# Three-operation rotary embeddings, and small tables moved from VectorE to GpSimd

## The chip, the cores and the metric

The kernel runs on one core of one Trainium2 chip. The metric is the device time of one execution in microseconds (us). Before the change it is 2278.96 us, the median of three runs (2276.32 to 2279.6).

The engines are named as in the profile: PE is TensorE's matmul, PEld its weight load, DVE is VectorE, ACT is ScalarE, POOL is GpSimd, SP is SyncE, which here issues the loads of weights. Each engine works through its own instructions in a fixed order.

## The reference

A decoder trunk of two layers over 256 rows of 2048 columns, in float32. One layer computes

```
h = RMSNorm(x)
[u | ret q,k,v,g | nsa q, 3 x (k,v), gates | diff q,k,v] = h @ W_in
x = x + concat[S5(u), Retention(q,k,v,g), NSA(q,...), DiffAttn(q,k,v)] @ W_out
x = x + relu(RMSNorm(x) @ W1)^2 @ W2
```

S5 is a state-space scan, the other three mixers are causal attentions with four heads of 128. The queries and keys get rotary embeddings:

```
ang = pos * theta ** (-arange(0, d, 2) / d)
rope(x) = [x1 * cos(ang) - x2 * sin(ang), x2 * cos(ang) + x1 * sin(ang)]
```

with x1 and x2 the two halves of a head. The retention's q and k and NSA's q have four heads of 128, the differential attention's q and k have eight heads of 64, and NSA's three keys (compressed, selected, window) have a single head of 128. The differential attention also needs one constant a layer, lambda = exp(sum(lq1 * lk1)) - exp(sum(lq2 * lk2)) + lam_init.

## The kernel before

The 256 rows are two row tiles (`NT` = 2) of 128 rows. Every large product goes through `product` (L157): for a block of 512 output columns it loads the weights in chunks of 128 x 1024 (`raw`, by SP's queue), ACT rounds a chunk to its high part (`wh`, L153), DVE subtracts to get the low part (`wl`, L154), and PE does twelve matmuls for it: eight with `wh` (L172, L173) and four with `wl` (L177). There are three buffers for `wh` and two for `wl`. So all through the kernel both ACT and DVE have one full chunk of work for each twelve matmuls.

A layer begins with `mixers` (L839): eleven products with W_in (u, then q, k, v of the differential attention, NSA's q and its key/value blocks with the gates, the retention's q, k, v, g), and between them the attentions and the S5 states (`s5_pair`, eight calls a layer, shared out over the steps by `PACE`). Everything that the mixers need of elementwise work lies on DVE and ACT, between the chunks. Then W_out and the two products of the MLP follow, with little elementwise work beside them.

The order of the instructions of each engine is laid by the framework's scheduler: it simulates the program, and takes what is ready by its place in the program, with blocks under `hp()` moved up by 350 places. That order is fixed when the program is built.

What the change touches:

- `rope` (L377 to L392): the rotary embedding of one row tile. It does five DVE operations: source times cos over the full width (L388), each half of the heads times sin into a scratch tile `rtmp` (L389, L390), and the subtraction and the addition into the two halves of the destination (L391, L392). It is called for both row tiles by `diff_tr`, `nsa_qt` and `ret_tr` (512 columns, five times a layer), and by `rope1_tr` for each single-head key (128 columns, three times a layer).
- `rope1_tr` (L658): ropes a single-head key of both row tiles, transposes them on PE and copies them out.
- `nsa_kv` (L635) and the `kcv` tiles (L883 on): copies of the key and value columns out of PSUM, one tile for each row tile.
- `rope_tables` (L280): cos and sin of all angles, 128 x 128 elements, once at the start: the angles, their turns (`turns`, L97) on DVE, then Sin on ACT (L295, L297).
- `diff_lambda` (L343): the constant `nlam` of each layer with `exp_small` (L118) on 4 columns.

POOL has little to do before: the causal masks and `rsqrt` (L81), a chain of fourteen small operations that gives each norm. Between the evacuation of u's product and the first head norm it has none.

Of the kernel before, what the change touches and what calls it, by code (L numbers as in the profile page):

```python
# [54 lines left out]
class Trunk:  # L55
# [18 lines left out]
    # ---------------------------------------------------------------- helpers  # L74
# [6 lines left out]
    def rsqrt(self, dst, v, n, tag):  # L81
        """dst = 1/sqrt(v + eps) on [rows, n] float32 columns, by Newton steps on GpSimd"""
# [11 lines left out]
    def rnd(self, dst, src):  # L94
        self.nc.vector.tensor_scalar(dst, src, MAGIC, -MAGIC, ALU.add, ALU.add)

    def turns(self, th, n):  # L97
        """th radians -> f1, f2 with f1 + f2 = th/(2 pi) less a whole number, |f1 + f2| <= 1/2."""
        V = self.nc.vector
# [6 lines left out]
        self.rnd(b, a)  # L106
# [4 lines left out]
        V.scalar_tensor_tensor(a, h, I2P[2], a, ALU.mult, ALU.add)  # L111
        V.tensor_tensor(f2, f2, a, ALU.add)
        V.tensor_tensor(a, f1, f2, ALU.add)
        self.rnd(b, a)
# [3 lines left out]
    def exp_small(self, dst, x, n):  # L118
        """dst = exp(x) to float32 rounding on few columns."""
        V = self.nc.vector  # L120
# [4 lines left out]
        V.scalar_tensor_tensor(r, k, -LN2_HI, r, ALU.mult, ALU.add)  # L125
        V.scalar_tensor_tensor(r, k, -LN2_LO, r, ALU.mult, ALU.add)
# [8 lines left out]
        V.scalar_tensor_tensor(dst, p, 1.0, e, ALU.add, ALU.mult)  # L135

    # ------------------------------------------------------- weights and products
# [19 lines left out]
    def product(self, chunks, lhs, n=512, before=None):  # L157
        """sum over k of lhs[k]^T @ w[k]; chunks hold two k each. Returns the PSUM tiles of both row tiles."""
# [36 lines left out]
    def to_slots(self, src, cols, slots, j0, gain=None):  # L195
        """src(t): token-major [128, >=cols] tiles; transposes cols into slot pairs from j0 on."""
# [83 lines left out]
    def rope_tables(self, posi, invf):  # L280
        nc = self.nc
        V = nc.vector
        posf = self.T(NT)
        V.tensor_copy(posf, posi)
        ang = self.T(NT * 64)
        for t in range(NT):
            V.tensor_scalar(ang[:, t * 64:(t + 1) * 64], invf, posf[:, t:t + 1], None, ALU.mult)
        f1, f2 = self.turns(ang, NT * 64)
        V.tensor_tensor(f1, f1, f2, ALU.add)
        self.rnd(f2, f1)  # L290
        V.tensor_tensor(f1, f1, f2, ALU.subtract)
# [69 lines left out]
    # ---------------------------------------------------------------- norm of the residual  # L361
# [14 lines left out]
    # ---------------------------------------------------------------- rotary and head norms  # L376
    def rope(self, dst, src, t, heads, d):  # L377
        """dst, src: [128, heads * d] token-major; dst must not be src."""
# [5 lines left out]
        tb = lambda tab: tab[:, t, ::step][:, None, :]  # L384
# [36 lines left out]
    def head_tr(self, src, dst, engine):  # L421
        """src(t): token-major [128, 4 * 128]; dst [128, 2, 4, 128] (row tile, head, row)"""
# [29 lines left out]
    def s5_table(self, i):  # L452
        """[128, 2, 256]: cos and sin of t * theta for the state column i."""
# [36 lines left out]
    def s5_pair(self, i):  # L490
        """pairs i and i + 1: the inputs go to the frame that rotates with theta, are summed there with
# [600 lines left out]
```

## Time and profile before

| | |
|---|---|
| median of three runs | 2278.96 us |
| profiled execution, first to last instruction (span) | 2274.8 us |
| PE busy | 2249.3 us (99%) |
| DVE busy | 1411.6 us (62%) |
| ACT busy | 1083.1 us (48%) |
| POOL busy | 144.7 us (6%) |

For the profiled execution the profile gives the span alone; the median of the timed runs is 4.2 us above it.

How to read it: the shares are means over stages with different limits. Each matmul's record lasts from its issue to the end of its result, so that the records of neighbours overlap and PE's share is high by nature. In the mixers (0 to 365 us and 1168 to 1505 us) DVE is much busier than in the rest. The same holds for DVE's records: an operation's record is longer than the distance to the next one's start in a full queue, and that distance is what the operation costs the queue.

### The profile page before, as it was taken

The numbers are of one execution on the slowest core, as the hardware profiler recorded it, in microseconds if no ns is written. First come the engines' busy times: TensorE is split into PE (matmuls) and PEld (weight loads), VectorE is DVE, ScalarE is ACT, GpSimd is POOL, SyncE is SP. The second block draws the span as 40 slices with busy tenths as digits, with TensorE's granted clock in tenths as the row PEclk, the third lists the DMA queues.
The fourth block names the chain that finished last, engine by engine and source line by source line (L and its number), as shares of the span: only waits on it lengthen the run. The fifth ranks groups of instructions, "written<-read, shape, count | busy, mean of one in ns | idle before, by whom it ended". The sixth has DMA issues, their size and how long they took to land.

```text
span 2274.8 us, 29209 instructions
## 1 busy us (share of the span) xinstructions
PE 2249.3 (99%) x10732; PEld 1831.1 (80%) x10732; DVE 1411.6 (62%) x2105; ACT 1083.1 (48%) x1410; POOL 144.7 (6%) x396
## 2 busy tenths in 40 slices
PE   8999999999999999999999999999999999999999
PEld 7777778888888888888877777888888888888887
DVE  8988975555555555455569997566554554555554
ACT  6456554544344344344545664445444443443443
POOL 0213111000000000000002212010000000000000
PEclk9999999999999999999999999999999999999999
DMA  7544735555655555555554456355555556556554
GB/s 252 165 133 130 241 113 167 183 182 191 194 185 192 190 192 185 195 186 185 186 175 155 131 152 206 120 178 183 186 192 189 190 181 201 187 190 191 191 194 167
DMA packets 115919, 409.62 MB, mean 180 GB/s; under 512 B 14016, under 2 KB 14272, under 8 KB 115776
## 3 DMA queue, kind: packets, MB, share of 16 engines
q1 hardware_dynamic: 113184, 405.06, 53.8%
q10 hardware_dynamic: 2592, 2.70, 0.3%
q8 instruction: 84, 1.38, 0.2%
q14 instruction: 59, 0.48, 0.1%
HBM read 405.61 MB, written 2.10 MB: 179 GB/s over the span
## 4 chain that ended last, share of the span: by engine, by line
PE 86%; DVE 7%; POOL 3%; issue 2%; ACT 2%; DMA 1%; DVEq 0%; ACTq 0%; SPq 0%
PE mm L177 27%; PE mm L172 27%; PE mm L173 27%; DVE wl L154 2%; PE tp L203 2%; DVE w L515 1%; PE glu L551 1%; POOL rst L89 1%; PE bu L502 1%; PE nsc L759 0%; PE yp L530 0%; PE npv L769 0%; POOL rst L91 0%; POOL rst L90 0%; PE cmp L693 0%
## 5 line engine op out<-in xcount | busy, mean ns | idle before, releaser
L153 ACT ACTIVATE wh<-raw 128x1024 fp32r<-128x1024 f32 (+1 forms) x752 | 790.5, 1052 | 1055.0 <-PE mm L173 944.7
L154 DVE TENSOR_TENSOR wl<-raw,wh 128x1024 fp32r<-128x1024 f32 (+1 forms) x752 | 908.0, 1213 | 594.5 <-PE mm L177 557.6
L172 PE MATMUL mm<-wh,Al 128*128 128x512 f32 (+1 forms) x1728 | 670.1, 389 | 1.9 <-ACT wh L153 1.5
L173 PE MATMUL mm<-wh,Ah 128*128 128x512 f32 (+1 forms) x1728 | 669.1, 388 | 0.0
L172 PE MATMUL mm<-wh,Bl 128*128 128x512 f32 x1280 | 498.4, 389 | 0.9 <-DVE Bl L213 0.9
L173 PE MATMUL mm<-wh,Bh 128*128 128x512 f32 x1280 | 498.4, 389 | 0.0
L177 PE MATMUL mm<-wl,Ah 128*128 128x512 f32 (+1 forms) x1728 | 466.9, 391 | 10.9 <-DVE wl L154 10.5
L177 PEld LDWEIGHTS mm<-wl,Ah 128*128 128x128 f32 x1728 | 316.0, 188 | 88.4 <-DVE wl L154 18.4
L172 PEld LDWEIGHTS mm<-wh,Al 128*128 128x128 f32 x1728 | 325.1, 188 | 73.2 <-issue 4.6
L173 PEld LDWEIGHTS mm<-wh,Ah 128*128 128x128 f32 x1728 | 325.2, 188 | 69.7 <-issue 5.6
L177 PE MATMUL mm<-wl,Bh 128*128 128x512 f32 x1280 | 344.2, 391 | 0.2 <-DVE wl L154 0.2
L172 PEld LDWEIGHTS mm<-wh,Bl 128*128 128x128 f32 x1280 | 240.3, 188 | 51.1 <-DVE Bl L213 1.1
L173 PEld LDWEIGHTS mm<-wh,Bh 128*128 128x128 f32 x1280 | 240.3, 188 | 49.7
L177 PEld LDWEIGHTS mm<-wl,Bh 128*128 128x128 f32 x1280 | 238.6, 188 | 49.0 <-DVE wl L154 0.6
L934 DVE TENSOR_TENSOR x<-mm,x 128x512 f32<-128x512 f32 x96 | 61.8, 686 | 105.5 <-PE mm L177 105.5
L213 DVE TENSOR_TENSOR Bl<-tp,Bh 128x512 fp32r<-128x512 f32 x76 | 52.1, 687 | 70.9 <-ACT Bh L212 70.9
L86 POOL TENSOR_SCALAR rv<-rv 128x2 f32<-128x2 f32 x4 | 1.0, 244 | 879.8 <-DVE rv L372 879.8
L987 ACT ACTIVATE hid<-mm,rb 128x512 f32<-128x512 f32 x64 | 40.6, 685 | 24.2 <-PE mm L177 24.2
L212 ACT ACTIVATE Bh<-tp 128x512 fp32r<-128x512 f32 x76 | 40.8, 584 | 5.7 <-PE tp L203 5.7
L988 DVE TENSOR_TENSOR hid<-hid 128x512 f32<-128x512 f32 x64 | 41.2, 684 | 0.0
L515 DVE TENSOR_TENSOR_SCAN w<-mag,z 128x256 f32<-128x256 f32 x64 | 40.7, 678 | 0.0
L218 DVE SCALAR_TENSOR_TENSOR Al<-tp,gains,Ah 128x256 fp32r<-128x256 f32 x64 | 29.3, 478 | 16.9 <-ACT Ah L217 16.9
(300 smaller groups left out, 1187.4 us busy)
## 6 DMA issues: line engine op xcount, KB each, us to landing
raw<-in_w_dram SPq DMA_DIRECT2D x512, 512.0 KB, 3.4
raw<-in_w_main_dram SPq DMA_DIRECT2D x160, 512.0 KB, 4.0
raw<-in_w_out_dram SPq DMA_DIRECT2D x64, 512.0 KB, 3.6
aux<-in_wcmp_dram SPq DMA_DIRECT2D x16, 512.0 KB, 5.2
raw<-in_w_gate_dram SPq DMA_DIRECT2D x16, 268.0 KB, 2.6
x<-in_x_dram SPq DMA_DIRECT2D x8, 256.0 KB, 5.1
aux<-in_s5g_dram SPq DMA_DIRECT2D x4, 512.0 KB, 4.8
out_dram<-x ACTq DMA_DIRECT2D x8, 256.0 KB, 2.1
```

The costliest lines, as they stand in the source:

```text
L153: self.nc.scalar.activation(h[:, :cols], r[:, :cols], AF.Copy)
L154: self.nc.vector.tensor_tensor(l[:, :cols], r[:, :cols], h[:, :cols].bitcast(F32), ALU.subtract)
L172: nc.tensor.matmul(acc[t], rows(xl, t), mov(wh, j), start=k == 0, stop=False)
L173: nc.tensor.matmul(acc[t], rows(xh, t), mov(wh, j), start=False, stop=False)
L177: nc.tensor.matmul(acc[t], rows(lhs[k][0], t), mov(wl, j), start=False, stop=k == nk - 1)
L203: nc.tensor.transpose(pt[:, kk, t * P:(t + 1) * P], src(t)[:, c:c + P], self.ident)
L212: nc.scalar.activation(h, pt, AF.Copy)
L213: nc.vector.tensor_tensor(l, pt, h.bitcast(F32), ALU.subtract)
L515: V.tensor_tensor_scan(w[:, c, :], mg, z[:, c, :], 0.0, ALU.mult, ALU.add)
L934: self.nc.vector.tensor_tensor(x, acc[t], x, ALU.add)
L987: nc.scalar.activation(h, acc[t], AF.Relu, scale=r[:, t:t + 1])
L988: V.tensor_tensor(h, h, h, ALU.mult)
```

## The change

The sine table gets twice the width, with the sign of each half in it: -sin for the first, +sin for the second. `rope` then does three operations over the full width: source times cos, the source with its halves swapped (a reversed step in the access pattern) times the signed sine, and their sum. `rope1` does the same three operations for the two row tiles of a single-head key at once; for that the key tiles of both row tiles become one tile (`ko`, `kcv`, `k1r`). In `rope_tables` and `diff_lambda` the elementwise work goes from DVE to POOL, the two row sums of `diff_lambda` excepted. [...] Docstrings and comments are dropped; that part is left out here.

```diff
-    def rnd(self, dst, src):
-        self.nc.vector.tensor_scalar(dst, src, MAGIC, -MAGIC, ALU.add, ALU.add)
+    def rnd(self, dst, src, V=None):
+        (V or self.nc.vector).tensor_scalar(dst, src, MAGIC, -MAGIC, ALU.add, ALU.add)
+
+    def mul_add(self, V, dst, a, k, b, t):
+        if V is self.nc.vector:
+            V.scalar_tensor_tensor(dst, a, k, b, ALU.mult, ALU.add)
+        else:
+            V.tensor_scalar(t, a, k, None, ALU.mult)
+            V.tensor_tensor(dst, t, b, ALU.add)
...
     def turns(self, th, n, V=None):
+        V = V or self.nc.vector
...
-        V.scalar_tensor_tensor(f2, h, I2P[1], f2, ALU.mult, ALU.add)
+        self.mul_add(V, f2, h, I2P[1], f2, c)
...
     def rope_tables(self, posi, invf):
-        V = nc.vector
+        G = nc.gpsimd
...
-        f1, f2 = self.turns(ang, NT * 64)
+        f1, f2 = self.turns(ang, NT * 64, G)
...
-        self.rs = self.cst.tile([P, NT, 64], F32, name="rs")
-        nc.scalar.activation(fl(self.rs), f1, AF.Sin, scale=TWO_PI)
+        self.rs = self.cst.tile([P, NT, 2, 64], F32, name="rs")
+        nc.scalar.activation(self.rs[:, :, 0, :], t3(f1), AF.Sin, scale=-TWO_PI)
+        nc.scalar.activation(self.rs[:, :, 1, :], t3(f1), AF.Sin, scale=TWO_PI)
...
     def diff_lambda(self, dl):
-        V = nc.vector
+        V = nc.gpsimd
...
-            V.tensor_reduce(sm[:, 2 * l:2 * l + 2], dl[:, l, 0::2, :], AX, ALU.add)
-        self.exp_small(ex, sm, n * 2)
+            nc.vector.tensor_reduce(sm[:, 2 * l:2 * l + 2], dl[:, l, 0::2, :], AX, ALU.add)
+        self.exp_small(ex, sm, n * 2, V)
...
     def rope(self, dst, src, t, heads, d):
-        cosb = tb(self.rc)[:, :, None, :].to_broadcast([P, heads, 2, h])
-        sinb = tb(self.rs).to_broadcast([P, heads, h])
+        cosb = self.rc[:, t, ::step][:, None, None, :].to_broadcast([P, heads, 2, h])
+        sinb = self.rs[:, t, :, ::step][:, None, :, :].to_broadcast([P, heads, 2, h])
         V.tensor_tensor(o, s, cosb, ALU.mult)
-        V.tensor_tensor(m[:, :, 0, :], s[:, :, 1, :], sinb, ALU.mult)
-        V.tensor_tensor(m[:, :, 1, :], s[:, :, 0, :], sinb, ALU.mult)
-        V.tensor_tensor(o[:, :, 0, :], o[:, :, 0, :], m[:, :, 0, :], ALU.subtract)
-        V.tensor_tensor(o[:, :, 1, :], o[:, :, 1, :], m[:, :, 1, :], ALU.add)
+        V.tensor_tensor(m, s[:, :, ::-1, :], sinb, ALU.mult)
+        V.tensor_tensor(dst, dst, tmp, ALU.add)
+
+    def rope1(self, dst, src):
+        V = self.nc.vector
+        tmp = self.wk.tile([P, 512], F32, name="rtmp", bufs=1)[:, :SEQ]
+        v4 = lambda x: x.rearrange("p t (b c) -> p t b c", b=2)
+        s, o, m = v4(src), v4(dst), tmp.rearrange("p (t b c) -> p t b c", t=NT, b=2)
+        V.tensor_tensor(o, s, self.rc[:, :, None, :].to_broadcast([P, NT, 2, 64]), ALU.mult)
+        V.tensor_tensor(m, s[:, :, ::-1, :], self.rs, ALU.mult)
+        V.tensor_tensor(o, o, m, ALU.add)
...
     def nsa_kv(self, acc, kcol, r, tag):
+        k = self.wk.tile([P, NT, P], F32, name="ko", tag="ko" + tag, bufs=1)
...
-                ko = self.wk.tile([P, P], F32, name="ko", tag="ko" + tag, bufs=2)
-                nc.scalar.activation(ko, acc[t][:, kcol * P:(kcol + 1) * P], AF.Copy, scale=r[:, t:t + 1])
+                nc.scalar.activation(k[:, t, :], acc[t][:, kcol * P:(kcol + 1) * P], AF.Copy, scale=r[:, t:t + 1])
...
     def rope1_tr(self, k, tag):
-        for t in range(NT):
-            o = self.wk.tile([P, P], F32, name="k1r", bufs=2)
-            self.rope(o, k[t], t, 1, P)
-            nc.tensor.transpose(pt[:, t * P:(t + 1) * P], o, self.ident)
+        o = self.wk.tile([P, NT, P], F32, name="k1r", bufs=1)
+        self.rope1(o, k)
+        for t in range(NT):
+            nc.tensor.transpose(pt[:, t * P:(t + 1) * P], o[:, t, :], self.ident)
...
-            kv = [self.wk.tile([P, 2 * P], F32, name="kcv", tag="ev", bufs=4) for _ in range(NT)]
+            kv = self.wk.tile([P, NT, 2 * P], F32, name="kcv", tag="ev", bufs=4)
```

`exp_small` takes the engine as `turns` does; on POOL its three multiply-and-add steps become two operations each.

## Rows read from the trace of the kernel before

**Rows 1.** The page: busy us, share, instructions; then a group: count, busy, mean ns, idle.

```profile
PE 2249.3 (99%) x10732; PEld 1831.1 (80%) x10732; DVE 1411.6 (62%) x2105; ACT 1083.1 (48%) x1410; POOL 144.7 (6%) x396
...
L154 DVE TENSOR_TENSOR wl<-raw,wh 128x1024 fp32r<-128x1024 f32 (+1 forms) x752 | 908.0, 1213 | 594.5 <-PE mm L177 557.6
```

**Rows 2.** Busy us of each engine (instructions) by stage, granted clock, DMA share, GB/s.

```profile
0.00:365.00 365.00, 351.44 (x1851) 271.65 (x1852) 306.13 (x733) 206.03 (x342) 67.64 (x192) 1.00 0.52 168
365.00:1168.00 803.00, 803.00 (x3645) 667.05 (x3644) 432.86 (x442) 361.80 (x417) 8.34 (x28) 1.00 0.57 189
1168.00:1505.00 337.00, 329.45 (x1782) 257.14 (x1781) 269.28 (x535) 181.15 (x284) 64.00 (x162) 1.00 0.47 152
```

**Rows 3.** The same view in windows of 20 us, some of both mixers.

```profile
40.00:60.00 20.00, 20.00 (x98) 15.50 (x98) 20.00 (x56) 8.84 (x14) 0.00 (x0) 1.00 0.56 178
80.00:100.00 20.00, 17.88 (x75) 13.52 (x73) 18.92 (x35) 10.42 (x15) 3.32 (x9) 0.91 0.46 138
...
1180.00:1200.00 20.00, 18.55 (x78) 13.61 (x79) 19.93 (x35) 10.25 (x14) 0.00 (x0) 1.00 0.40 127
...
1420.00:1440.00 20.00, 20.00 (x96) 15.42 (x96) 10.42 (x29) 9.15 (x12) 2.92 (x3) 1.00 0.34 110
```

**Rows 4.** Who waited for whom, whole span: us in total, times, longest.

```profile
PEld mm L177 <- DVE wl L154: 18.9, 22, 2.3
PE mm L177 <- DVE wl L154: 10.7, 14, 1.8
```

**Rows 5.** DVE in order of time, single stretches: start us, us, what.

```profile
84.19 0.69 DVE L388 TENSOR_TENSOR drp<-evr,rc 128x512 f32<-128x512 f32 x1
84.79 0.69 DVE L517 TENSOR_TENSOR sc<-w,cs 128x512 f32<-128x512 f32 x1
...
1358.66 0.22 DVE L392 TENSOR_TENSOR k1r<-k1r,rtmp 128x64 f32<-128x64 f32 x1
1358.79 0.28 DVE L388 TENSOR_TENSOR k1r<-ko,rc 128x128 f32<-128x128 f32 x1
1358.99 0.42 DVE L681 TENSOR_TENSOR xp<-vcT,pe 128x256 f32<-128x256 f32 x1
1359.33 0.22 DVE L389 TENSOR_TENSOR rtmp<-ko,rs 128x64 f32<-128x64 f32 x1
```

**Rows 6.** DVE at the start: the tables' first operation, a later one, one of lambda.

```profile
8.88 0.16 DVE L284 CAST scr<-posi 128x2 f32<-128x2 int32 x1
...
23.03 0.21 DVE L95 TENSOR_SCALAR scr<-scr 128x128 f32<-128x128 f32 x1
23.16 0.17 DVE L122 TENSOR_SCALAR scr<-scr 128x32 f32<-128x32 f32 x1
...
34.51 0.15 DVE L125 SCALAR_TENSOR_TENSOR scr<-scr 128x4 f32<-128x4 f32 x1
34.58 0.17 DVE L130 TENSOR_SCALAR scr<-scr 128x32 f32<-128x32 f32 x1
```

**Rows 7.** ACT in order of time, where it takes the tables over.

```profile
25.79 0.32 ACT L295 ACTIVATE rs<-scr 128x128 f32<-128x128 f32 x1 [0.54 <-DVE scr L291]
...
26.64 1.05 ACT L153 ACTIVATE wh<-raw 128x1024 fp32r<-128x1024 f32 x1
```

**Rows 8.** POOL in order of time, the first head norm: first and last operations.

```profile
70.74 1.17 POOL L86 TENSOR_SCALAR hv<-hv 128x16 f32<-128x16 f32 x1 [46.53 <-DVE hv L406]
...
78.53 0.20 POOL L91 TENSOR_SCALAR rst<-rst 128x16 f32<-128x16 f32 x1
78.81 0.22 POOL L92 TENSOR_TENSOR hc<-hc,rst 128x16 f32<-128x16 f32 x1
```

**Rows 9.** POOL and DVE in order of time, a mask beside a chunk's low part.

```profile
301.49 0.64 POOL L563 TENSOR_SCALAR_AFFINE_SELECT np<-np 128x512 f32<-128x512 f32 x1 [1.76 <-ACT np L761]
301.64 1.56 DVE L154 TENSOR_TENSOR wl<-raw,wh 128x1024 fp32r<-128x1024 f32 x1 [0.28 <-ACT np L761]
```

**Rows 10.** DVE in order of time, the first differential query's norm.

```profile
79.07 1.29 DVE L410 TENSOR_TENSOR evr<-evr,hc 128x512 f32<-128x512 f32 x2 [2.49 <-POOL hc L92]
```

More of the change, by code (lines that the diff above doesn't have):

```diff
@@ L92, in rsqrt, with turns @@
             G.tensor_tensor(dst, dst, t, ALU.mult)
-    def rnd(self, dst, src):
-        self.nc.vector.tensor_scalar(dst, src, MAGIC, -MAGIC, ALU.add, ALU.add)
-    def turns(self, th, n):
-        V = self.nc.vector
+    def rnd(self, dst, src, V=None):
[6 more added lines that the diff above has]
+            V.tensor_tensor(dst, t, b, ALU.add)
+    def turns(self, th, n, V=None):
+        V = V or self.nc.vector
         c, h, l, a, b, f1, f2 = (self.T(n) for _ in range(7))
@@ L105, in turns, with exp_small @@
         V.tensor_scalar(a, h, I2P[0], None, ALU.mult)
-        self.rnd(b, a)
+        self.rnd(b, a, V)
         V.tensor_tensor(f1, a, b, ALU.subtract)
         V.tensor_scalar(f2, l, I2P[0], None, ALU.mult)
-        V.scalar_tensor_tensor(f2, h, I2P[1], f2, ALU.mult, ALU.add)
+        self.mul_add(V, f2, h, I2P[1], f2, c)
         V.tensor_scalar(a, l, I2P[1], None, ALU.mult)
-        V.scalar_tensor_tensor(a, h, I2P[2], a, ALU.mult, ALU.add)
+        self.mul_add(V, a, h, I2P[2], a, c)
         V.tensor_tensor(f2, f2, a, ALU.add)
         V.tensor_tensor(a, f1, f2, ALU.add)
-        self.rnd(b, a)
+        self.rnd(b, a, V)
         V.tensor_tensor(f1, f1, b, ALU.subtract)
         return f1, f2
-    def exp_small(self, dst, x, n):
-        V = self.nc.vector
+    def exp_small(self, dst, x, n, V=None):
+        V = V or self.nc.vector
         k, r, p, e = (self.T(n) for _ in range(4))
@@ L124, in exp_small @@
         V.tensor_scalar(k, k, -MAGIC, None, ALU.add)
-        V.scalar_tensor_tensor(r, k, -LN2_HI, r, ALU.mult, ALU.add)
-        V.scalar_tensor_tensor(r, k, -LN2_LO, r, ALU.mult, ALU.add)
+        self.mul_add(V, r, k, -LN2_HI, r, e)
+        self.mul_add(V, r, k, -LN2_LO, r, e)
         V.tensor_scalar(p, r, 1.0 / 5040.0, 1.0 / 720.0, ALU.mult, ALU.add)
@@ L134, in exp_small @@
         V.tensor_scalar(e.bitcast(I32), k, 8388608.0, None, ALU.mult)
-        V.scalar_tensor_tensor(dst, p, 1.0, e, ALU.add, ALU.mult)
+        if V is self.nc.vector:
+            V.scalar_tensor_tensor(dst, p, 1.0, e, ALU.add, ALU.mult)
+        else:
+            V.tensor_scalar(p, p, 1.0, None, ALU.add)
+            V.tensor_tensor(dst, p, e, ALU.mult)
     def raw(self, src, cols=1024):
@@ L281, in rope_tables @@
         nc = self.nc
-        V = nc.vector
+        G = nc.gpsimd
         posf = self.T(NT)
-        V.tensor_copy(posf, posi)
+        G.tensor_copy(posf, posi)
         ang = self.T(NT * 64)
         for t in range(NT):
-            V.tensor_scalar(ang[:, t * 64:(t + 1) * 64], invf, posf[:, t:t + 1], None, ALU.mult)
-        f1, f2 = self.turns(ang, NT * 64)
-        V.tensor_tensor(f1, f1, f2, ALU.add)
-        self.rnd(f2, f1)
-        V.tensor_tensor(f1, f1, f2, ALU.subtract)
+            G.tensor_scalar(ang[:, t * 64:(t + 1) * 64], invf, posf[:, t:t + 1], None, ALU.mult)
+        f1, f2 = self.turns(ang, NT * 64, G)
+        G.tensor_tensor(f1, f1, f2, ALU.add)
+        self.rnd(f2, f1, G)
+        G.tensor_tensor(f1, f1, f2, ALU.subtract)
         self.rc = self.cst.tile([P, NT, 64], F32, name="rc")
-        self.rs = self.cst.tile([P, NT, 64], F32, name="rs")
-        fl = lambda x: x.rearrange("p t d -> p (t d)")
-        nc.scalar.activation(fl(self.rs), f1, AF.Sin, scale=TWO_PI)
+        self.rs = self.cst.tile([P, NT, 2, 64], F32, name="rs")
+        t3 = lambda x: x.rearrange("p (t d) -> p t d", t=NT)
+        nc.scalar.activation(self.rs[:, :, 0, :], t3(f1), AF.Sin, scale=-TWO_PI)
+        nc.scalar.activation(self.rs[:, :, 1, :], t3(f1), AF.Sin, scale=TWO_PI)
         nc.scalar.activation(f2, f1, AF.Abs)
-        nc.scalar.activation(fl(self.rc), f2, AF.Sin, scale=-TWO_PI, bias=self.half_pi)
+        nc.scalar.activation(self.rc.rearrange("p t d -> p (t d)"), f2, AF.Sin, scale=-TWO_PI, bias=self.half_pi)
     def s5_params(self, s5p):
@@ L639, in nsa_kv @@
         c = self.sm.tile([P, NT], F32, name="kc", tag="kc" + tag, bufs=2)
[L640 removed]
+        k = self.wk.tile([P, NT, P], F32, name="ko", tag="ko" + tag, bufs=1)
+        vv = []
         with self.hp():
             for t in range(NT):
[L643 to L645 removed]
+                nc.scalar.activation(k[:, t, :], acc[t][:, kcol * P:(kcol + 1) * P], AF.Copy, scale=r[:, t:t + 1])
                 vo = self.wk.tile([P, P + 1], F32, name="vo", tag="vo" + tag, bufs=2)
@@ L652, in nsa_kv @@
             junk = self.wk.tile([P, P], F32, name="kjunk", tag="djunk", bufs=2)
-            nc.scalar.activation(junk, k[t], AF.Square, scale=P ** -0.5, accum_out=v[:, t:t + 1])
+            nc.scalar.activation(junk, k[:, t, :], AF.Square, scale=P ** -0.5, accum_out=v[:, t:t + 1])
         self.rsqrt(c, v, NT, "k" + tag)
@@ L883, in mixers @@
         with self.hp():
-            kv = [self.wk.tile([P, 2 * P], F32, name="kcv", tag="ev", bufs=4) for _ in range(NT)]
+            kv = self.wk.tile([P, NT, 2 * P], F32, name="kcv", tag="ev", bufs=4)
             for t in range(NT):
-                nc.scalar.activation(kv[t], a[t][:, :2 * P], AF.Copy, scale=r[:, t:t + 1])
-        kcT = self.rope1_tr([x[:, :P] for x in kv], "c")
+                nc.scalar.activation(kv[:, t, :], a[t][:, :2 * P], AF.Copy, scale=r[:, t:t + 1])
+        kcT = self.rope1_tr(kv[:, :, :P], "c")
         pt = self.misc("vc")[:, :SEQ]
         for t in range(NT):
-            nc.tensor.transpose(pt[:, t * P:(t + 1) * P], kv[t][:, P:], self.ident)
+            nc.tensor.transpose(pt[:, t * P:(t + 1) * P], kv[:, t, P:], self.ident)
         vcT = self.wk.tile([P, SEQ], F32, name="vcT", bufs=1)
```

3 lines of the change are left out of this document (removed).

## The prediction

> **What bounds the kernel now.** I read the page's busy times first: PE is busy for 99% of the span [rows 1], but each matmul's record lasts longer than its turn, so this share says only that PE is seldom empty, not that it is fed at full rate. The second view, busy time by stage, tells more [rows 2]. Weight loads (PEld) have short records and serve as a measure of rate. In the MLP stretch PEld is busy 667.05 of 803 us, 83.1%, and PE has no gap; in the mixers of layer 0 it is 271.65 of 365 (74.4%) and in those of layer 1 257.14 of 337 (76.3%). At the MLP's rate these loads would take 271.65 / 0.831 = 327 us and 257.14 / 0.831 = 309 us: the mixers lose at most 38 and 28 us, 66 us together (an upper bound: the attentions' and states' matmuls have fewer loads for their time). This is all that any relief of DVE can win, since outside the mixers DVE has 432.86 of 803 us to do. Third, the windows of 20 us: DVE is full or nearly so from 40 us on and again at 1180 us (20.00, 18.92, 19.93 of 20), but half idle late in the mixers (10.42 at 1420 us) [rows 3]. Fourth, the waits: PE and its loads wait for DVE's low parts `wl` for 10.7 and 18.9 us, one and the same cause seen at two queues [rows 4]. So the change works on the right engine, in a place where PE hangs on it, but only for part of the time.
>
> **The change part by part.** In a full queue DVE's cost of an operation is the distance between starts, not the record. From neighbours in the trace: 0.60 us for 512 columns, 0.13 for 64, 0.20 for 128, 0.34 for 256 [rows 5].
>
> Full-width ropes. Before 0.60 + 4 x 0.34 = 1.96 us, after 3 x 0.60 = 1.80: 0.16 saved. Two row tiles, five uses a layer, two layers are 20 calls: 3.2 us. The records alone (0.69 and 0.42) would promise twice as much; that is the trap of reading durations here. The swapped halves are a reversed step over an outer dimension; the half-width products of before already read strided halves at the plain price (0.22 for 64 columns, L389 as L392 [rows 5]), so I take no surcharge; at 10% on one of three operations the saving of 0.16 would fall to 0.10.
>
> Single-head ropes. Before 2 x (0.20 + 4 x 0.13) = 1.44, after 3 x 0.34 = 1.02: 0.42 saved, six calls, 2.5 us. Both row tiles must now be there before the first operation; ACT evacuates them one right behind the other, so the wait is one evacuation at most, and it has DVE's other work to hide it.
>
> Tables and lambda. DVE loses 21 table operations: 11 with two tensors at 0.20, 7 with one at 0.13 (23.03 to 23.16 [rows 6]), two angle products that I put at 0.16 (between the costs of 64 columns with two inputs and of 128) and a copy at 0.07: 3.5 us. Of lambda's 29 operations 27 go, 25 of them on a few columns at 0.07 (34.51 to 34.58 [rows 6]) and two at 0.20: 2.2 us. Together 5.7 us, all near the start of layer 0 (the first at 8.88, lambda's under way at 34.5 [rows 6]). On ACT one Sin of 0.32 us more [rows 7], beside PE's work.
>
> DVE's queue thus gets 3.2 + 2.5 + 5.7 = 11.4 us shorter. What of it reaches the end? The differential q and k and NSA's q (12 of 20 full calls) and the compressed and selected keys (4 of 6 single ones) lie in the stretches where DVE is full: 12 x 0.16 + 4 x 0.42 = 3.6 us, taken in full. The retention's ropes and the window key come where DVE has slack like that at 1420 us: nothing. The tables' 5.7 us lie where PE itself is busy for 20.00 of 20 us [rows 3]; there they only bring forward the S5 work that DVE still has in hand, which pays from 60 to 110 us, where PE does stall. I count half, 2.8 us.
>
> The price on POOL. No two-input operation of 128 columns on POOL is in the trace. From below, one of 16 columns costs 0.28 from start to start [rows 8]; from above, a mask of 512 columns records 0.64 [rows 9], 0.72 with the same gap. Between them by columns, a one-input operation of 128 gets 0.38, and I put a two-input one at 0.48, twice the column part. The tables become 23 operations on POOL (12 with one input, 11 with two): 9.8 us free, 6 to 17 by the ends. POOL idles until u's norm and again for 46.53 us until 70.74 [rows 8]; lambda's 30 operations (8.4 us at 0.28) fit there too. But POOL isn't free while DVE works: of the fourteen operations of the first head norm, all alike in their work, the first records 1.17 us and the last two 0.20 and 0.22, and the chain takes 79.03 - 70.74 = 8.3 us where 14 x 0.28 = 3.9 would do, a factor of 2.1 [rows 8]. And the other way round: a `wl` that begins 0.15 us into a mask records 1.56 [rows 9] instead of its mean 1.21 [rows 1]: 0.35 lost. The 23 table operations are shorter than the mask; if a third of them catch DVE at 0.2 us each that is 1.6 us, and if all of them catch it at 0.35, 8.0. I take 1.6, since the wide ones need a third to a half of the mask's time and DVE's PSUM and small operations lie between the two-input ones.
>
> The Trainium skill speaks against this part: "SBUF — State Buffer" (SBUF: two separate sides) has DVE and GpSimd share a port pair under an exclusive lock, so that a DVE operation with two SBUF inputs and a GpSimd one block each other for a whole instruction. By that rule rows 8 and 9 are the same thing seen from both sides, and the trace agrees; what it would do to the time is the slower rival below.
>
> Sum: 3.6 + 2.8 - 1.6 = 4.8 us off the profiled 2274.8, that is 2270.0; the median of the timed runs lies 4.2 us above the profiled span, so 2274.2, rounded to 2274.
>
> **Rivals.** *All of it counts, and more.* Every us of the 11.4 comes off the path, since the low parts are late in the stretches where DVE is full. In addition the stall near 85 us goes, where PE ran out of low parts and the granted clock then fell: its mean is 0.91 from 80 to 100 us [rows 3], so 2.4 GHz for most of the window and 1.2 for some of it, and 0.09 x 20 = 1.8 us are lost. 2279.0 - 13.2 = 2266. For it speaks that DVE waits 2.49 us there for a norm from POOL and is behind ever after [rows 10]; against it, that this very wait comes from POOL, which gets more work.
>
> *Hidden.* DVE's savings go into its own waiting, since ACT, DVE and PE hand each other buffers and PE is never long empty: 2278 to 2279, no change. For it speaks that the waits that name DVE outright are 18.9 us in the whole span [rows 4], a third of what the mixers lose; against it DVE's full windows.
>
> *POOL late: slower.* ACT takes the tables over at 25.79 us, with a chunk's `wh` right behind it in its queue [rows 7]. On POOL the tables begin at about 9 us (8.88 on DVE [rows 6]). With the factor 2.1 they take 9.8 x 2.1 = 20.6 us, and if u's norm, fourteen more operations, is laid between them, 3.9 to 8.3 us more: ready at 34 to 38 us, 8 to 12 us after today's. If the plan keeps the Sin where it is, ACT stands there, and PE has two chunks of 2.6 us in hand (twelve matmuls of 803 / 3645 = 0.22 us each, the MLP stretch's spacing [rows 2]): 3 to 7 us lost. With up to 8.0 us of DVE held and the ropes' 3.6 won back, 2279 + 7 + 8 - 3.6 = 2290 at the worst and some 2285 in the middle. It decides once the tables end later than 25.8 + 5.2 = 31 us. Against it: free of DVE they'd be done at 19, and the planner may set the Sin later, as no rope comes before the first head norm has been applied at 79 us [rows 10].
>
> *A new order.* The scheduler lays all of it anew; the two layers' mixers do the same work and lose 38 and 28 us, so order and start are worth several us either way. This is no case of its own, it widens all of them by about 4.
>
> **How the numbers follow.** A measurement here tells 0.2%, 4.6 us, from no change. The forecast (2270 to 2278) has a chance of 0.40, half of it below that bound; all of it counts 0.20; hidden 0.18; POOL late 0.22. Faster 0.20 + 0.20 = 0.40, same 0.20 + 0.18 = 0.38, slower 0.22. The range reaches from 2264 (the second case less 2) to 2287 (the middle of the slow case and 2).
>
> **What would show it.** In the changed kernel's trace a full-width rope should show three DVE starts 0.60 apart, a single-head one three at 0.34, and DVE's records some 20 us fewer in all (in queue time 11.4). POOL should show 53 more operations before 60 us, the wide ones at 0.3 to 0.5 and some over 1 us beside a `wl`. If ACT's idle time before the Sin of the tables is over 2 us, or DVE waits for the norm of the first head longer than 2.49 us, POOL is late and I am wrong. If layer 1, where no table work is, gains nothing, the ropes' 3.6 us are wrong; if the gain there is far over 2 us, it is the order and not the work.

## The result, and the profile after

The changed kernel takes 2291.28 us (median of four runs, 2289.57 to 2293.13) against 2279.28 us for the kernel before, measured beside it (2276.32 to 2280.39): ratio 1.0061, 95% interval 1.0048 to 1.0074. It is slower by 0.6%, and it lies above the range of the prediction. The profiled execution's span is 2291.4 us, 16.6 above the 2274.8 of before. That is more than the 12.0 us between the medians: each kernel was profiled in one execution, and that of after was the longest of its four. The stages below are of these two executions, and 4.6 of their 16.6 us are the scatter from one execution to the next.

The first part of the page of the kernel after answers to [rows 1]; its columns are busy time, share and instructions.

```profile
PE 2253.6 (98%) x10732; PEld 1834.7 (80%) x10732; DVE 1401.5 (61%) x1975; ACT 1085.6 (47%) x1413; POOL 168.7 (7%) x449
```

DVE is busy for 10.1 us less. The relief is there, and the time went up all the same.

To see where, I take the first matmul of each large product as a milestone (its start in the trace, by line and order) and cut the execution there: the first matmul of all, the product of u up to the first product of the differential queries ("u's product"), from there to the first matmul of W_out in layer 0, and the same stretch in layer 1. The rest hardly differs: from W_out to the second layer's u it is 818.3 to 818.5 us in every kernel below, u's product in layer 1 takes 22.7, and the tail 820.4 to 822.9 us.

| us | first matmul | u's product | mixers, layer 0 | mixers, layer 1 | clock lost | span |
|---|---|---|---|---|---|---|
| before | 7.69 | 25.92 | 292.50 | 287.27 | 1.7 | 2274.8 |
| after | 8.81 | 33.10 | 294.03 | 292.98 | 10.2 | 2291.4 |
| difference | +1.1 | +7.2 | +1.5 | +5.7 | +8.5 | +16.6 |

The remaining 1.1 us are in the tail. "Clock lost" is read from the granted clock in windows of 5 us in the mixers: 5 us times (1 - clock), summed over all windows below 0.97. It is contained in the stretches, not added to them, and it is of one execution: the 61 timed executions of the kernel before have a median of 2276.3 us where the granted clock over the whole span is 1.000 (19 of them), 2278.4 at 0.999 (28) and 2280.7 at 0.998 (14). So the same program loses more or less by the clock from one execution to the next.

*The start.* The same view by stage and by 5 us windows (time, busy us of PE, PEld, DVE, ACT, POOL with instructions, granted clock, DMA share, GB/s); after first, then the windows of before.

```profile
20.00:25.00 5.00, 5.00 (x29) 4.17 (x28) 5.00 (x28) 3.14 (x4) 4.43 (x8) 1.00 1.04 408
25.00:30.00 5.00, 3.22 (x17) 2.31 (x14) 2.61 (x9) 1.44 (x7) 4.42 (x13) 1.00 0.86 296
30.00:35.00 5.00, 3.50 (x9) 2.49 (x10) 4.66 (x19) 3.97 (x9) 1.77 (x7) 0.67 0.03 13
35.00:40.00 5.00, 5.00 (x16) 3.95 (x15) 3.23 (x17) 1.96 (x4) 3.54 (x12) 0.65 0.55 155
```

```profile
25.00:30.00 5.00, 4.58 (x21) 3.49 (x20) 5.00 (x22) 4.43 (x9) 0.00 (x0) 1.00 0.66 243
30.00:35.00 5.00, 5.00 (x23) 4.11 (x24) 5.00 (x28) 2.42 (x3) 0.00 (x0) 1.00 0.69 210
35.00:40.00 5.00, 5.00 (x28) 4.25 (x27) 5.00 (x32) 3.41 (x7) 0.00 (x0) 1.00 0.41 134
```

From 25 to 30 us PE, DVE and ACT are busy for 3.22, 2.61 and 1.44 of 5 us while POOL is nearly full (4.42): three engines stand behind the fourth. The waits of after between 20 and 44 us say behind what (engine, line, whom it waited for: us in total, times, longest):

```profile
PEld mm L184 <- DVE Al L230: 4.1, 2, 2.4
...
ACT rs L308 <- POOL scr L304: 3.6, 1, 3.6
PE mm L184 <- DVE Al L230: 3.3, 2, 2.0
DVE Al L230 <- ACT Ah L229: 2.4, 1, 2.4
```

And in order of time (start us, us, what, idle before it and whom it waited for), POOL, ACT, DVE and PE of after:

```profile
11.50 1.75 POOL L109 TENSOR_SCALAR scr<-scr 128x128 f32<-128x128 f32 x1
13.34 0.49 POOL L110 TENSOR_TENSOR scr<-scr 128x128 f32<-128x128 f32 x1
13.91 0.41 POOL L111 TENSOR_TENSOR scr<-scr,scr 128x128 f32<-128x128 f32 x1
...
15.55 0.53 POOL L102 TENSOR_SCALAR scr<-scr 128x128 f32<-128x128 f32 x1
...
23.63 1.12 POOL L86 TENSOR_SCALAR rv<-rv 128x2 f32<-128x2 f32 x1
...
28.11 0.45 POOL L304 TENSOR_TENSOR scr<-scr 128x128 f32<-128x128 f32 x1
...
31.08 0.20 POOL L92 TENSOR_TENSOR ra<-ra,rst 128x2 f32<-128x2 f32 x1
```

```profile
23.76 1.28 ACT L308 ACT_TABLE_LOAD   x1
28.60 0.31 ACT L308 ACTIVATE rs<-scr 128x128 f32<-128x128 f32 x1 [3.56 <-POOL scr L304]
...
29.22 0.45 ACT L229 ACTIVATE Ah<-tp,gains 128x256 fp32r<-128x256 f32 x1
```

```profile
29.70 0.48 DVE L230 SCALAR_TENSOR_TENSOR Al<-tp,gains,Ah 128x256 fp32r<-128x256 f32 x1 [2.39 <-ACT Ah L229]
...
31.31 0.40 DVE L864 TENSOR_SCALAR rh<-ra 128x2 f32<-128x2 f32 x1 [0.27 <-POOL ra L92]
31.62 0.47 DVE L230 SCALAR_TENSOR_TENSOR Al<-tp,gains,Ah 128x256 fp32r<-128x256 f32 x1
```

```profile
25.63 0.40 PE L184 MATMUL mm<-wh,Al 128*128 128x512 f32 x1
25.87 0.40 PE L185 MATMUL mm<-wh,Ah 128*128 128x512 f32 x1
...
30.24 0.50 PE L184 MATMUL mm<-wh,Al 128*128 128x512 f32 x1 [2.02 <-DVE Al L230]
...
32.71 0.79 PE L184 MATMUL mm<-wh,Al 128*128 128x512 f32 x1 [1.25 <-DVE Al L230]
33.30 0.63 PE L185 MATMUL mm<-wh,Ah 128*128 128x512 f32 x1
33.73 0.63 PE L184 MATMUL mm<-wh,Al 128*128 128x512 f32 x1
```

Read from the bottom up. The tables' last operation on POOL ends at 28.56 (L304); the Sin, which ran at 25.79 before [rows 7], waits for it. Behind the Sin in ACT's queue stands the rounding of the transposed activations (`Ah`, L229), which DVE needs for their low part (`Al`, L230) and PE for its next matmul. So PE idles 2.02 us. The norm of u shares POOL with the tables: its first operation starts at 23.63, its last ends at 31.28, and DVE's queue stands at `rh` (L864, half of that norm) until 31.31; before, `rh` was reached at 24.25 (line below). PE idles another 1.25 us. After that the granted clock is 0.67 and 0.65: 1.2 instead of 2.4 GHz for about two thirds of 10 us. The matmuls show it: starts 0.24 us apart at 25.63, 0.43 apart at 33.30. PE's idle time in u's product is 2.02 + 1.25 = 3.3 us, where before had one wait of 0.42, so 2.9 us more; with the clock's (0.33 + 0.35) x 5 = 3.4 us that makes 6.3 of the 7.2 us that u's product lost. The other 0.9 lie in its first matmuls, which start 0.43 us apart until 14.1 us here and until 9.6 before; no experiment bears on them.

```profile
24.25 0.17 DVE L844 TENSOR_SCALAR rh<-ra 128x2 f32<-128x2 f32 x1 [0.83 <-POOL ra L92]
```

*Layer 1*, where no table is made, is the second part. Windows of after in layer 1, the three places where the clock falls:

```profile
1250.00:1255.00 5.00, 2.73 (x10) 1.98 (x9) 4.92 (x7) 1.06 (x1) 0.04 (x1) 0.86 0.34 107
1255.00:1260.00 5.00, 5.00 (x20) 3.99 (x19) 5.00 (x9) 1.06 (x1) 0.00 (x0) 0.79 0.35 131
1340.00:1345.00 5.00, 3.15 (x17) 2.91 (x15) 5.00 (x10) 2.14 (x3) 1.38 (x3) 0.74 0.36 103
1345.00:1350.00 5.00, 5.00 (x29) 4.26 (x28) 4.56 (x9) 2.89 (x4) 0.00 (x0) 0.92 0.65 225
1415.00:1420.00 5.00, 4.91 (x38) 2.35 (x38) 0.85 (x6) 1.14 (x4) 0.04 (x1) 0.75 0.51 191
1420.00:1425.00 5.00, 5.00 (x21) 3.51 (x19) 2.76 (x5) 3.13 (x5) 0.63 (x1) 0.91 0.09 14
```

Each pair loses (0.14 + 0.21) x 5 or about 1.7 us, 5.1 together, nearly the size of the 5.7 that layer 1 lost; the kernel before has no window below 0.97 in layer 1. It is not the whole account: PE also idles there for 3.3 us more than before (10.9 in all), and the rest of the stretch is 2.8 us shorter. What PE did ahead of them, in order of time:

```profile
1252.56 1.19 PE L189 MATMUL mm<-wl,Ah 128*128 128x512 f32 x4 [2.27 <-DVE wl L166]
```

```profile
1342.20 1.12 PE L189 MATMUL mm<-wl,Ah 128*128 128x268 f32 x4 [1.85 <-DVE wl L166]
```

```profile
1415.09 0.48 PE L772 MATMUL npv<-cvo,npc 15*128 15x129 f32 x2 [1.26 <-POOL npc L767]
```

Here each fall came after a wait of 1.3 to 2.3 us and cost as much again. Over the whole span PE's waits for `wl` grew from 10.7 to 14.3 us, the longest from 1.8 to 2.3 [rows 4]; the same work is done in another order. Whether the two belong together is for the experiments.

```profile
PE mm L189 <- DVE wl L166: 14.3, 16, 2.3
```

### The profile page after: what moved, and what is told of

The parts are those of the page before. It is cut to its first block, busy times and chain, and to the rows that moved or that the text cites. A ratio compares the mean times of both kernels' runs of the same rounds, so it can differ in the third digit from the quotient of the medians.

```text
span 2291.4 us, 29152 instructions
## 1 busy us (share of the span) xinstructions
PE 2253.6 (98%) x10732; PEld 1834.7 (80%) x10732; DVE 1401.5 (61%) x1975; ACT 1085.6 (47%) x1413; POOL 168.7 (7%) x449
## 4 chain that ended last, share of the span: by engine, by line
PE 86%; DVE 4%; POOL 2%; issue 1%; ACT 1%; DMA 1%; DVEq 0%; ACTq 0%
PE mm L189 27%; PE mm L184 26%; PE mm L185 26%; PE tp L215 2%; DVE wl L166 1%; PE yp L551 1%; PE bu L523 1%; DMA aux<-in_wcmp_dram 1%; PE glu L572 1%; POOL rst L89 1%; PE nsc L779 0%; DVE w L536 0%; PE npv L789 0%; POOL npc L767 0%; PE cmp L713 0%
## 5 line engine op out<-in xcount | busy, mean ns | idle before, releaser
L189 PE MATMUL mm<-wl,Ah 128*128 128x512 f32 (+1 forms) x1728 | 469.0, 393 | 14.1 <-DVE wl L166 14.1
L230 DVE SCALAR_TENSOR_TENSOR Al<-tp,gains,Ah 128x256 fp32r<-128x256 f32 x64 | 29.4, 477 | 20.0 <-ACT Ah L229 19.9
```

Of the source, the lines that this page charges most:

```text
L189: nc.tensor.matmul(acc[t], rows(lhs[k][0], t), mov(wl, j), start=False, stop=k == nk - 1)
```

## Experiments

All were measured beside the kernel before, whose medians were 2277.8 to 2278.6 us. The table has the stages as above, of one profiled execution each; "POOL" says what of tables (T), lambda (L) and the half norm `rh` is on POOL. The expectations name the start of the differential q's product (dq); the table has u's product, which is that start less the first matmul's, since the first matmul itself starts anywhere from 7.55 to 10.17 us in these kernels.

| kernel | ropes | POOL | median | ratio (95%) | u's product | layer 0 | layer 1 | clock lost |
|---|---|---|---|---|---|---|---|---|
| e1_ropes_only | new | | 2283.01 | 1.0022 (1.0013–1.0032) | 26.07 | 290.98 | 292.11 | 3.4 |
| e2_tables_only | old | T L | 2292.53 | 1.0068 (1.0055–1.0080) | 32.88 | 296.87 | 290.73 | 8.5 |
| e4_lambda_only_pool | new | L | 2275.24 | 0.9990 (0.9981–0.9998) | 26.43 | 283.89 | 292.98 | 1.7 |
| b2_lambda_old_ropes | old | L | 2279.64 | 1.0005 (0.9996–1.0014) | 27.24 | 287.20 | 291.20 | 1.7 |
| e3_sin_later | new | T L | 2292.76 | 1.0068 (1.0055–1.0082) | 32.08 | 295.56 | 293.03 | 8.5 |
| e7_rh_only | new | T L rh | 2286.81 | 1.0038 (1.0025–1.0051) | 31.03 | 289.89 | 292.62 | 3.4 |
| e6_both_waits_gone | new | T L rh | 2285.39 | 1.0032 (1.0020–1.0045) | 27.18 | 294.25 | 288.91 | 5.1 |
| e5_behind_norm | new | T L | 2296.14 | 1.0081 (1.0067–1.0095) | 26.43 | 302.76 | 292.16 | 10.2 |
| e8_lambda_rh_pool | new | L rh | 2279.22 | 1.0003 (0.9994–1.0012) | 26.07 | 287.79 | 291.57 | 3.4 |
| e9_pool_load_only | new | L rh + load | 2281.05 | 1.0009 (1.0001–1.0018) | 26.99 | 288.05 | 291.74 | 3.4 |
| b4_ropes_swapped | old | | 2275.27 | 0.9985 (0.9976–0.9993) | 27.15 | 289.43 | 287.66 | 0.0 |

**Which part costs.** The first kernel has the new ropes with tables and lambda on DVE, the second the old ropes with both on POOL, the third the new ropes with lambda alone on POOL, the fourth the same with the old ropes.

```diff
# e1, in the kernel after (rope_tables, diff_lambda)
-        G = nc.gpsimd
+        G = nc.vector
-        V = nc.gpsimd
+        V = nc.vector
# e2, in the kernel before (with the engine argument of the helpers)
-        V = nc.vector
+        G = nc.gpsimd
...
-        V = nc.vector
+        V = nc.gpsimd
...
-        self.exp_small(ex, sm, n * 2)
+        self.exp_small(ex, sm, n * 2, V)
...
# e4 in after, b2 in e2 (rope_tables alone)
-        G = nc.gpsimd
+        G = nc.vector
```

> The changed ropes alone (three operations, joined key tiles), tables and lambda on VectorE as before. Theory (the tables on GpSimd come late and hold ScalarE at the start, some 8 us; the rest of the loss, 1.5 us in layer 0 and 6.6 in layer 1, is the new order of instructions): the dq product starts within 1 us of before's 33.6 us; the total is 2275 to 2285, with the mixers of layer 1 off before's by several us either way. Rival (the ropes themselves cost: reversed step, joined tiles): the start is as before, but the mixers of layer 1 lose the same 6 to 7 us as in the changed kernel, total 2287.

> Tables and lambda on GpSimd alone, ropes with five operations as before. Theory: the dq product starts some 8 us late, as in the changed kernel (41.9 us); layer 1 has the work of before but another order, so its mixers may differ from before's by several us; total 2283 to 2292. Rival (ropes cost): the start is 8 us late and layer 1 is equal to before within 1 us, total 2287.

> The whole change without the tables' part: tables on VectorE, lambda on GpSimd, new ropes. Theory: lambda has nobody who waits for it until 180 us, so the start is as in the ropes-only kernel within 1 us, and the total differs from that by the order alone (up to some 5 us). Rival (any work on GpSimd holds VectorE): the start is 2 to 4 us later than in the ropes-only kernel.

> Lambda on GpSimd, tables on VectorE, ropes with five operations as before: against the kernel with lambda on GpSimd and the new ropes (2275.2) it gives the ropes' share. Theory (ropes shorten VectorE's queue by 5.7 us, 3.6 of them on the path, and the order scatters each layer by several us): 2276 to 2284, slower than 2275.2. Rival (the ropes cost, the gain is lambda's): 2272 or less.

Every kernel with the tables on DVE has u's product at 26.1 to 27.2 us, before's own being 25.92; with them on POOL and nothing else done it is 32.9 and 33.1, with old ropes or new. The tables on POOL are the loss at the start, and the ropes have no part in it. Lambda on POOL costs nothing there (26.43 and 27.24).

For the ropes the pairs disagree: 2275.24 against 2279.64 with lambda on POOL (4.4 us won), 2291.28 against 2292.53 with both (1.2 won), 2283.01 against 2277.93 with neither (5.1 lost). The same operations, but each kernel is laid anew.

How much a new order alone is worth can be read in layer 1, by comparing the instructions of PE, DVE, ACT and POOL one by one. The 13 kernels have only four orders there. Before and b4 share one, but for b4's swapped lines (287.27 and 287.66 us); e2 and b2 share another, with the operations of before one for one (290.73 and 291.20); e1, e4, e5, e7, e8 and e9 a third (291.57 to 292.98); after, e3 and e6 the fourth (292.98, 293.03 and 288.91). So two kernels with old ropes and a new order lie 3.5 to 3.9 us above before's, 1.7 of it clock. But one and the same order also gives 288.91 and 293.03: in e6 PE idles 8.6 us instead of the 10.9 of after and loses 3.4 instead of 5.1 by the clock. Most of what layer 1 lost in the profile of after is thus not fixed by its order. And the rival that the ropes or their joined key tiles cost something there (old ropes 287.3 to 291.2, new 288.9 to 293.0) is not excluded.

**The two waits at the start.** e3 ties the Sin behind u's evacuation, by a bias of zero made from it on POOL; e7 takes `rh` out of DVE's queue; e6 does both, with the zero made on ACT; e5 ties the tables behind the norm of u instead (a zero made from the norm is added to the positions) and the Sin as in e6.

```diff
# e3 (e6, e5: the zero by nc.scalar.activation(..., AF.Copy, scale=0.0))
+        nc.gpsimd.tensor_scalar(self.zb, u[0][:, 0:1], 0.0, None, ALU.mult)
-        nc.scalar.activation(self.rs[:, :, 0, :], t3(f1), AF.Sin, scale=-TWO_PI)
+        nc.scalar.activation(self.rs[:, :, 0, :], t3(f1), AF.Sin, scale=-TWO_PI, bias=self.zb)
...
# e6, e7
-        V.tensor_scalar(rh, r, 0.5, None, ALU.mult)
+        nc.gpsimd.tensor_scalar(rh, r, 0.5, None, ALU.mult)
# e5
+        G.tensor_scalar(zr, r, 0.0, None, ALU.mult)
+        G.tensor_tensor(posf, posf, zr, ALU.add)
```

> The whole change, but ScalarE's Sin of the tables is tied behind the evacuation of u's product by a zero bias made from u (one small GpSimd operation more), so ScalarE can't wait for GpSimd in the middle of the first product; all engines keep the changed kernel's order from there on. Theory: 6 to 8 us come back at the start, the dq product starts at 34 to 36 us, the rest is unchanged, total 2283 to 2286. Rival (the loss at the start is VectorE held at the shared memory port, or u's norm being late behind the tables): nothing comes back, total 2289 or more.

> The whole change with rh alone moved to GpSimd; ScalarE's Sin stays where the scheduler puts it. Theory (two waits side by side, either is enough): the Sin still holds ScalarE for 3 us or more, the dq product starts at 39 to 42 us. Rival (rh alone is the cause): it starts at 34 to 35 us. The rest of the order is new, so the total says little: 2284 to 2294.

> The whole change with both waits taken from the queues at the start: rh is halved on GpSimd itself, and ScalarE's Sin is tied behind u's evacuation by a zero bias that ScalarE makes itself. TensorE's order is that of the changed kernel but for the first product. Theory: 7 to 8 us come back and stay, the dq product starts at 34 to 35 us, the total is 2283 to 2285 (the changed kernel's order keeps its other 8 us of loss). Rival (VectorE held by GpSimd's wide operations): the dq product still starts at 37 us or later, total 2287 or more.

> The whole change, with the tables' operations on GpSimd tied behind u's norm (the positions get zero times the norm added) and ScalarE's Sin tied behind u's evacuation, by a zero bias that ScalarE makes itself. Theory (the loss at the start is two waits at once for GpSimd: ScalarE's Sin for the tables, and VectorE's halving of the norm, rh, for u's norm, which GpSimd does behind the tables): neither is late, the dq product starts at 33.6 to 35 us, the total is that of the kernels with the tables on VectorE, 2274 to 2284, by its order. Rival (GpSimd's wide operations hold VectorE wherever they run): the start is right, but the dk product (before 57.9) and the dv product (82.4) start 3 us late or more.

Each wait alone is enough to hold PE. e3 gave back 1.0 us at the start and nothing in the median, as its rival had it: with the Sin out of the way, DVE stands at `rh`, and PE idles longer than in the changed kernel (in order of time, DVE and PE of e3):

```profile
30.40 0.40 DVE L871 TENSOR_SCALAR rh<-ra 128x2 f32<-128x2 f32 x1 [3.77 <-POOL ra L92]
```

```profile
31.82 0.79 PE L184 MATMUL mm<-wh,Al 128*128 128x512 f32 x1 [4.53 <-DVE Al L230]
```

With `rh` out of the way (e7), ACT stands at the Sin for the same 3.56 us, and u's product takes 31.03. With both gone (e6) it takes 27.18, one PE wait of 0.59 us is left, and the clock stays at 1.00 to 40 us (ACT of e7, then PE of e6):

```profile
27.38 0.31 ACT L308 ACTIVATE rs<-scr 128x128 f32<-128x128 f32 x1 [3.56 <-POOL scr L304]
```

```profile
29.48 0.50 PE L184 MATMUL mm<-wh,Al 128*128 128x512 f32 x1 [0.59 <-DVE Al L230]
```

So there are two waits side by side, not in series, which together cost 33.10 - 27.18 = 5.9 us. The median falls by 5.9 us too (2291.28 to 2285.39), but that the two agree is partly chance: the spans of the two profiled executions differ by 9.6 us, since layer 1 takes 4.1 less in e6. Its dq product starts at 35.96 us, one later than expected and one before the rival's 37.

Taking both waits away leaves e6 7.6 us slower than the kernel before beside it. By stages it lies less in layer 1 (288.91) than in layer 0, 294.25 us, where the kernels with lambda on POOL and the tables on DVE (e4, b2, e8, e9) take 283.9 to 288.1. All with the tables on POOL lie above that (289.9 and more): PE idles for 10.6 to 16.3 us in their layer 0 and for 4.9 to 7.5 in all others. What makes them wait there, the tables' lateness or the order that came with it, no kernel separates.

e5 fell outside what was expected: its start is good (26.43), but now the tables begin later, and it is again the Sin that stands in ACT's queue, with the S5 pair's `ut` and a chunk behind it (ACT, then PE of e5, and PE's windows):

```profile
51.77 0.40 ACT L318 ACTIVATE rs<-scr,zb 128x128 f32<-128x128 f32 x1 [7.03 <-POOL scr L307]
```

```profile
54.23 2.84 PE L533 MATMUL bu<-ut,s5b 32*128 32x256 f32 x16 [4.16 <-ACT ut L518]
```

```profile
50.00:55.00 5.00, 0.84 (x7) 0.71 (x8) 2.69 (x6) 3.23 (x8) 4.25 (x13) 0.92 0.61 210
55.00:60.00 5.00, 5.00 (x23) 3.67 (x18) 4.82 (x11) 2.97 (x5) 2.21 (x10) 0.50 0.36 108
```

PE is busy for 0.84 of 5 us, then runs at 1.2 GHz throughout the next 5. I had moved the wait, not removed it. A likely reason, not tested, is that the scheduler places the Sin where its simulation has POOL done, and POOL takes longer.

**The load on POOL without the waits, and order alone.** e8 is e4 with `rh` on POOL; e9 adds 23 operations on POOL, as many and as wide as the tables', whose result nobody reads; b4 is the kernel before with two lines of `rope` swapped.

```diff
# e8, in e4
-        V.tensor_scalar(rh, r, 0.5, None, ALU.mult)
+        nc.gpsimd.tensor_scalar(rh, r, 0.5, None, ALU.mult)
# e9, in e8
+        for t in range(NT):
+            G.tensor_scalar(a[:, t * 64:(t + 1) * 64], invf, 1.0, None, ALU.mult)
+        for i in range(10):
+            G.tensor_scalar(b, a, 0.5, None, ALU.mult)
+            G.tensor_tensor(a, a, b, ALU.subtract)
+        G.tensor_tensor(a, a, b, ALU.add)
...
# b4, in before
-        V.tensor_tensor(o, s, cosb, ALU.mult)
         V.tensor_tensor(m[:, :, 0, :], s[:, :, 1, :], sinb, ALU.mult)
         V.tensor_tensor(m[:, :, 1, :], s[:, :, 0, :], sinb, ALU.mult)
+        V.tensor_tensor(o, s, cosb, ALU.mult)
```

> New ropes, lambda on POOL, tables on DVE, and rh (half of u's norm) on POOL instead of DVE. Theory: rh was held up only where POOL's norm was late, which it is not here, so this gives 2274 to 2277, as without it (2275.2), and the first diff q product starts at 33.5 to 34.5 us. Rival: rh in DVE's queue costs by itself; then over 2 us less, 2273 or below.

> The same, and POOL does besides 23 operations of 128 columns at the start (12 with one input, 11 with two, as many and as wide as the tables' on POOL in the changed kernel, on a scratch of their own) whose result nobody reads; the real tables stay on DVE. Theory: the price of tables on POOL is the waits behind them, and what they take from DVE by sharing is 1.5 to 2 us, so the first diff q product starts at 34 to 36 us and the whole is 2275 to 2280 with the order's scatter. Rival: the load on POOL is itself the price; then diff q starts at 39 us or later and the whole is 2283 or more.

> The kernel before with the order of rope's products in the text swapped (sine products ahead of the cosine product): the same operations in number and size, laid by the scheduler in another order on DVE. Theory: order alone moves the time by several us; then it differs from 2278 by over 2 us one way or the other. Rival: order is worth next to nothing, and equal work gives 2277 to 2279.

e8 came out at 2279.22, above what was expected and 2.7 us above e4 by the spans (2275.5 and 2272.8). Layer 0 takes 3.9 us more (287.79 against 283.89), 1.7 of it one fall of the clock, and layer 1, whose order is the same, 1.4 less; a cause in `rh` is not seen. e9 has the PE order of e8 in all these stretches, and is above it by 0.9 us in u's product and 1.8 in the median. Neither is clear of the scatter: b4, with nothing more on POOL than before has, takes 27.15 for u's product, and e9's median lies within e8's runs (2275.33 to 2283.04). So the load itself costs about 1 us at the start, a fraction of the 5.9 us of the waits, and the rival's price (dq at 39 us or later) did not come. b4 is inconclusive on order: PE's order hardly differs, layer 1 takes 287.66 against 287.27, the spans are equal (2274.9 and 2274.8), yet the timed ratio is 0.9985 (0.9976 to 0.9993). Much of that goes with the clock: b4's granted clock is 1.000 in eight of eleven executions, in those of before beside it in eight of 27; among these the medians are 2274.6 and 2275.8. I draw no more from it than that about 0.15% between two kernels of nearly equal order needs no cause in the work. e4's 0.10% gain on before is thus no more than a tie; it is the fastest form of the change that was run, and it leaves the tables on DVE.

**The clock.** Over the 13 kernels, one profiled execution of each, the loss by the granted clock comes in steps of about 1.7 us: 0 in b4, 1 in before, e4 and b2, 2 in e1, e7, e8 and e9, 3 in e6, 5 in e2 and e3, 6 in after and e5. Of the 32 falls in the mixers, 30 lie near a wait of PE of 1.2 us or more (from 3 us before its end to 5 us behind it). But a wait does not always bring one: of the 79 such waits 32 have a fall near them, of the 31 of 2 us or more 15. The same wait for the first attention's probabilities, 3.26 us in layer 1, brought one in e1 and e9 and none in e4 and e7. In size the falls match the difference of after and before in layer 1 (5.1 of 5.7 us), but not other differences: e4 and e7 have one such step in layer 1 and take 292.98 and 292.62 us, e6 has two and takes 288.91. No kernel was run that takes away a single wait of layer 1 on purpose, so the share of the clock there rests on the traces alone.

## Why the prediction was wrong

It was wrong in sign and in size: 4.8 us were to be won, and 12.0 were lost. Step by step, as it stood:

*Where the time is bound* held: DVE's windows are full early, and where PE stands still it is mostly behind DVE or what DVE waits for.

*The ropes' operations* cost what was worked out. In the kernel after the starts, at 118 us in DVE's order of time, are 0.60 us apart for the cosine and the reversed step alike:

```profile
118.37 0.68 DVE L401 TENSOR_TENSOR drp<-evr,rc 128x512 f32<-128x512 f32 x1
118.97 0.68 DVE L402 TENSOR_TENSOR rtmp<-evr,rs 128x512 f32<-128x512 f32 x1
119.58 0.68 DVE L401 TENSOR_TENSOR drp<-evr,rc 128x512 f32<-128x512 f32 x1
```

So there is no surcharge for the swapped halves, and DVE's busy time fell by 10.1 us where 11.4 were taken off its queue. (Of the sign that I gave, some 20 us less by records: the sum of DVE's records fell from 1527.3 to 1504.9 us, by 22.4; the page's busy time counts overlapping records once.) That 3.6 us of it reach the end is not shown: e4 against b2 has 4.4, other pairs 1.2 and -5.1, and layer 1 gains nothing in any kernel.

*The tables' half of 5.7 us* was not separated. It was to pay from 60 to 110 us, in layer 0. There the four kernels with lambda off DVE and the tables on it take 283.9 to 288.1 us, and those with tables and lambda on DVE (before, e1, b4) 289.4 to 292.5, so some relief may be in it; but their order differs, and with the tables off DVE too the stretch is longer (289.9 to 302.8).

*The price on POOL* is the step that failed. It counted 1.6 us, for operations of DVE held up by POOL's. As far as it went nothing speaks against it: e9 measures 0.9 and 1.8. But the tables on POOL cost 7.2 us in u's product alone, of which 5.9 came back when ACT and DVE no longer waited for POOL there (e6). The step treated POOL's idle time as room, and asked how long POOL would work and not who waits for POOL in order. Two do. The Sin was named, in the rival "POOL late", with its lateness priced too high (tables at 34 to 38 us, in truth 28.6) and its condition too mild: it was to decide only if the tables ended after 31 us, since PE had two chunks in hand. They ended at 28.56 and PE had been dry since 28.2, because behind the Sin stood not the next `wh` but five `Ah`, without which the chunks in hand can't be used. The second, DVE's `rh` behind the norm of u, I had read only as a delay of the tables. And the cost of a wait left out the clock: 3.3 us of idle time at the start brought 3.4 us at 1.2 GHz. I had seen the like in the kernel before at 85 us and booked it as a gain for one rival, not as a price that a new wait can have. This step covers about half of the loss; the rest, in layer 0 and layer 1, has no cause that the runs separate.

The signs that were to show POOL late all came: ACT idle for 3.56 us before the Sin (the bound was 2), and DVE waiting 3.41 us for the first head norm, where it was 2.49 [rows 10]:

```profile
87.97 1.29 DVE L431 TENSOR_TENSOR evr<-evr,hc 128x512 f32<-128x512 f32 x2 [3.41 <-POOL hc L92]
```

*A new order* was given 4 us for both layers. Layer 1 alone spans 287.3 to 293.0 us over the 13 kernels, layer 0 with the tables on DVE 283.9 to 292.5. The order of before, which b4 shares, has the shortest layer 1 of the four that were seen, so each of the others lost there; the range should have been wider upward, and the chance of slower well above 0.22.

*The 4.2 us* between the profiled span and the median, which the sum adds, are no fixed distance: the timed executions of before lie 1.7 to 2.2 us above their own spans, and the rest is that the profiled execution of before was a quick one (a span of 2274.8 us, where the 61 executions have a median of 2276.3).

## What to carry to other kernels

Before work goes to an idle engine, find the first consumer of each result and of whatever else is queued on that engine, and list what stands behind those consumers in their own queues: here the price was in ACT's and DVE's queues, not on POOL. Work the moment at which it decides out from the operand that PE needs next, not from the chunks in flight. Where the order is laid by a scheduler, build the same work in a few orders, profile each more than once, and take their spread as the least that a change must win; and reckon that a wait of PE of a us or two may cost as much again by the clock, as it did beside 32 of 79 such waits here.

## What was not expected of the hardware

On POOL the one-input operation of 128 columns was the slower one: 0.53 to 0.68 us by records (L102 at 15.55, L95) against 0.41 to 0.49 for two inputs (L110, L111), where I had taken 0.38 and 0.48 from start to start. The Trainium skill would have it the other way round ("GPSIMD Engine Reference", Engine selection: one-input work runs at about line rate, two-input work about half as fast as on VectorE). On VectorE the one-input operation took 0.21 us [rows 6], so here it was the one-input work that fell behind; the measurement decides.

Five of POOL's operations up to 28.56 us took 0.7 to 1.2 us more than their like (L109 at 11.50 recorded 1.75), each begun while DVE ran one of its `wl`, whose record is 1.21 us. That agrees with the Trainium skill, "SBUF — State Buffer" (SBUF: two separate sides), where the loser of the shared ports blocks for the other's whole instruction. What DVE loses by it is less: u's product is 0.9 us longer in e9 than in e8.

The granted clock fell to 0.5 after waits of PE as short as 1.3 to 2.3 us, and each fall cost about 1.7 us or twice that. Yet more than half of the waits of that size left it at 1.00, and in e6 it fell at 1321.5 us with no wait of over 0.44 us near.
